# Two transformer blocks on one NeuronCore: GpSimd's block of convolution channels is projected first, and 62 instead of 27 of VectorE's convolution taps stand ahead of the attention

## The chip, the core and the metric

The kernel runs on 1 core of one Trainium2 chip. The time is device microseconds (us) from launch to end. Engines by their names in the profile: PE is TensorE, PEld its weight loads, DVE is VectorE, ACT is ScalarE, POOL is GpSimd, SP is SyncE, which issues most DMAs. Lower is better.

## What is computed

The reference applies two blocks to a sequence of 512 tokens of width 1024, in float32. The change lies in the first mixer of the first block: a gated causal depthwise convolution of 31 taps beside an attention with forget gates.

```python
h = rmsnorm(x, norm_mix_g[l])
proj = h @ w_in[l]
u_glu, q, k, v, f_logit, gate_c, gate_a = jnp.split(proj, cuts, axis=-1)
...
a, gate = jnp.split(u_glu, 2, axis=-1)
u = a * jax.nn.sigmoid(gate)
u = conv(u, dw_w, 31 taps, causal, one filter per channel) + dw_b
u = silu(layernorm(u)) @ pw_w
...
s = q k^T * scale + c_i - c_j        # c: running sum of log sigmoid(f_logit)
p = softmax(s, causal);  o = p @ v   # 8 heads of 64
x = x + (sigmoid(gate_c) * u + sigmoid(gate_a) * (o @ attn_branch_w)) @ w_out
```

After it come a cross attention, a mixture of 16 experts, and a second block with a mixer, a cross attention and a feed-forward layer. None of that is touched.

## The kernel before, in words

Every float32 product is made of three float32r products: a weight chunk (128x1024, brought by DMA to `wraw`) is split into an upper part `wh` (ACT, line 126) and a lower part `wl` (DVE, line 127), and PE multiplies upper by upper, upper by lower and lower by upper (lines 112 to 114). Of `wh` and `wl` there are three buffers each, so that a chunk can be split when PE has done with the chunk three before it. Each projection of 128 columns is 24 such products of 512 columns.

Mixer 1 (`mixer1`) goes through these stages. The norm of the input and the first projections stand in an order written out by hand (`first_norm`). Then come, for each of four blocks `m` of 128 convolution channels, the projections of `a` and of `gate`; ACT takes the tanh of the gate (line 725) and DVE multiplies it with `a` to give `cu` (line 726). The values of the attention follow (four accumulators in PSUM, taken to `v` by ACT and by DVE's line 127), then the forget gates (`fz`, `fc`, lines 754 to 762), then the queries and keys of the first pair of heads, then the attention.

The convolution is made a tap at a time (`conv31`). Three blocks run on DVE: the first tap with the bias is line 919, the other 30 are line 927, each reading `cu` and the sum `acc` and writing `acc`, all in SBUF. Block 3 runs on GpSimd: line 919, and then 30 times a product (line 924, to `pr`) and a sum (line 925, to `acc`). The taps of DVE come from a generator, `taps`, that the code draws on at three places: a number of taps after the forget gates, some in every step of the attention (`some_taps`, after the maximum of that step's scores), and the rest at the end.

The attention has 32 steps (8 heads by 4 blocks of 128 queries), run by `interleave`: a step makes the scores on PE (lines 987 and 988), DVE adds the mask (line 1005), adds the decay and takes the maximum (line 1008), ACT takes the exponential (line 1015), DVE normalises (lines 1017 and 1018), and two steps later PE transposes the result (line 1036). Between the steps PE makes further projections (queries, keys, gates), 14 products to a step.

PSUM has four buffers named `mm` for projections; they go round. The third and fourth accumulators of the values take the buffers of the last block's `a` and `gate`, so that they wait for that block's `cu`.

Outside `first_norm` the rows of each engine are put in order by a scheduler when the kernel is built; every engine then runs its own rows strictly in that order and waits on semaphores. So a row that is late holds up all rows behind it on its engine.

```python
ps0 = first_norm(k, xp, xs, hT, wj, [CU, CU + 512, CU + P])
...
for _ in islice(taps, 27):
    pass
...
def some_taps(s):
    with k.issue_after(k.scored):
        for _ in islice(taps, 2):
            pass
```

Of the kernel before, what the change touches and what calls it, by code (L numbers as in the profile page):

```python
# [27 lines left out]
RAW_BUFS = 4  # weight chunks on their way  # L28
PART_BUFS = 3  # weight chunks in two parts
# [4 lines left out]
class HL:  # L34
    """A float32 value held as the exact sum of two float32r parts."""
# [11 lines left out]
class Stack:  # L47
    """An HL [P, K, T] in tiles of two K each, of the size of a weight chunk."""
# [11 lines left out]
def rev_blocks(ap, n, w=P):  # L60
    """The last dimension (n * w) of a 2-d view, read as n blocks in reverse order."""
    return bass.AP(
        tensor=ap.tensor,
        offset=ap.offset + (n - 1) * w,
        ap=[list(ap.ap[0]), [-w, n], [1, w]],
    )
# [6 lines left out]
class Ctx:  # L73
# [24 lines left out]
    def iota(self, pool, name, shape, pattern, mult):  # L98
        """A float32 tile of base-0 iota values."""
        i = pool.tile(shape, I32, name=name + "i")  # L100
        self.nc.gpsimd.iota(i, pattern=pattern, base=0, channel_multiplier=mult)
        f = pool.tile(shape, FT, name=name)
        self.nc.gpsimd.tensor_copy(f, i)
        return f
# [11 lines left out]
    def mm2(self, out, a, b, first, last):  # L116
        """Products of both parts of b by a, which holds upper and lower parts side by side."""
        nc = self.nc
        nc.tensor.matmul(out, a, b.hi, start=first, stop=False)
        return nc.tensor.matmul(out, a, b.lo, start=False, stop=last)  # L120
# [25 lines left out]
    def ring(self, name, pools):  # L146
        """The next of the pools with its number of buffers, each taken as often as it has them."""
# [8 lines left out]
    def load_w(self, parts, a, c, raws=None, ws=None):  # L156
        """Brings a weight chunk [P, a, c] to the chip, in two parts.

        parts: (slice of the chunk, DRAM view) pairs that together fill it. raws, ws: pools and
        their numbers of buffers to take in turn."""  # L160
# [19 lines left out]
    def load_cols(self, wv, c0):  # L180
        """128 columns of a weight view [P, K, C]."""
        return self.load_w([(None, wv[:, :, c0 : c0 + P])], wv.shape[1], P)

# [19 lines left out]
    def transpose_rows(self, dst, hn, t):  # L203
        """hn [P tokens, D] -> dst[:, j, t-th 128 columns], row p of j holding feature 8p+j."""
# [7 lines left out]
    def turn_job(self, dst, hn, t):  # L212
        """transpose_rows in two steps: the transposes with the upper parts, and the lower parts."""
# [19 lines left out]
    def proj_T(self, w, hT, n):  # L233
        """psum [128 columns of the chunk w, n tokens]."""
# [6 lines left out]
    def proj_job(self, wv, c0, hT, n, evac):  # L241
        """proj_T of 128 columns of a weight view in two halves, then evac(psum)."""
# [14 lines left out]
    def load_rows(self, wv, k0, c0):  # L257
        """Two rows (one at the end of an odd K) and 512 columns of a weight view [P, K, C]."""
# [3 lines left out]
    def proj_rows_job(self, src, nt, wv, evac, pre=(), late=False):  # L262
        """src [P, K, nt*128] (features on partitions) times wv [P, K, C]: evac(t, c0, psum).

        pre: the first chunks, if they have been loaded. late: take the results of 512 columns
        after half of the products of the next."""
# [27 lines left out]
    def proj_x(self, src, wv, mid=None, end=None, also=None):  # L294
        """Adds the products of src [P, K, T] and wv [P, K, D] to x. The last chunks are taken by
        token tile, so that what follows on the first tiles can begin: mid(t) runs after a tile's
        first of these, end(t) after its last. also: a job to do after some of the first
        products."""
# [24 lines left out]
    def proj_norm_head(self, src, wv, g, pool, dst, cols, also=None):  # L323
        """proj_x, the norm of x with the features on partitions in dst, and head() of that."""
# [27 lines left out]
    def head(self, ws, hT, after={}):  # L352
        """proj_T of a few weight chunks, the first half of the tokens before the second.

        after: what is to run after a half (0, 1) of a chunk (0, ...). The results are left in
        PSUM."""
# [10 lines left out]
    def load_x(self, src):  # L367
        """Brings the residual stream [T, D] on chip."""
# [15 lines left out]
    def mem_norm(self, mem, mem_g, room, short):  # L384
        """The memory, normalised, in two tiles of room(). short(): a tile for a short time."""
# [11 lines left out]
    def mem_turn(self, mT, hns):  # L397
        """Puts the memory to mT with the features on partitions, as a job."""
# [4 lines left out]
    def cross_kv(self, pool, mT, wk, wv):  # L403
        """Keys and values of the memory (512 columns), the values as a job to be done."""
# [23 lines left out]
    def cross_attn(self, pool, src, w_prev, free, kv, gain_ap, wq, hd, more=(), also=None):  # L428
        """Adds the products of src and w_prev to x, and gives the heads' outputs of the
        attention to the memory, in pool(). free: to be called when src has been read. kv() gives  # L430
        keys, values and the job that makes these. more: jobs that can be done meanwhile. also: as
        in proj_x."""
# [108 lines left out]
class MemoryKV:  # L541
    """Keys and values (1024 columns) of the memory mT, left in DRAM, in steps.

    room: a tile [P, M] or [P, 512] for a result on its way."""
# [11 lines left out]
    def split_k(self, lo=None):  # L556
        """Brings and splits the next 128 columns of w_k."""
# [4 lines left out]
    def keys(self, room):  # L562
        """The keys of the columns that have waited longest."""
# [3 lines left out]
    def load_v(self, i0, i1, raw, queue=None):  # L567
        """Brings chunks of w_v."""
# [5 lines left out]
    def split_v(self, n=1, lo=None):  # L574
        """Splits the next chunks of w_v; only PART_BUFS may wait for their products."""
# [17 lines left out]
class RowNorm:  # L593
    """The norm of x by token tiles in steps, with the features on partitions in dst."""
# [19 lines left out]
class Feed:  # L614
    """it, with n items taken before they are needed."""
# [19 lines left out]
def ahead(it, n):  # L635
    """it, with n items taken before they are needed."""
# [8 lines left out]
def interleave(steps, lags, jobs, per_step, done, also=None):  # L645
    """Attention steps with other products between them.

    A step is the jobs that its stages need to be done, and a list of stages, each of which needs
    the results of the one before; stage i is issued lags[i] steps after the first, so that the
    chain between them runs meanwhile. jobs yields what it has issued, in products. also(s) runs  # L650
    in every step."""
# [22 lines left out]
def mixer1(k, wide, late):  # L674
    """The sum of the gated branches; wide() makes its place; late() runs near its end."""
# [4 lines left out]
    with ExitStack() as st:  # L680
        hp = st.enter_context(k.sb("m1h", bufs=1))
        hT = k.pair(hp, [P, KD, T], "hT")
        with k.sb("m1x", bufs=1, side="right") as xp:
            xs = [xp.tile([P, D], FT, name=f"xin{t}") for t in range(NT)]
            with k.tc.manual_schedule(engines={*MANUAL, E.Pool, E.SP}):
                ps0 = first_norm(k, xp, xs, hT, wj, [CU, CU + 512, CU + P])
# [3 lines left out]
        # per-channel vectors of the convolution, brought to [channel, value]  # L690
# [24 lines left out]
        with ExitStack() as s2:  # L715
            ap = s2.enter_context(k.sb("m1a", bufs=1))
            # gated unit, transposed: channels on partitions
            us = []
            for m in range(4):
# [7 lines left out]
                us.append(u)  # L727
# [10 lines left out]
            # values, tokens on partitions  # L738
            vt = Values(k, ap, "v")
            k.proj_rows(hT, NT, wj[:, :, CV : CV + 512], lambda t, c0, ps: vt.put(t, ps))  # L740
            # forget gates: running sum of log sigmoid, negated
# [25 lines left out]
            for _ in islice(taps, 27):  # L767
                pass
# [37 lines left out]
            def some_taps(s):  # L806
                with k.issue_after(k.scored):
                    for _ in islice(taps, 2):
# [5 lines left out]
        with ExitStack() as s3:  # L814
# [4 lines left out]
            def branch(b, src, m0):  # L819
                """Two times 128 output channels of a branch, with their gates."""  # L820
# [6 lines left out]
            # layer norm over the channels: to tokens, normalise, and back  # L827
# [34 lines left out]
            # branches, gates and their sum  # L862
# [11 lines left out]
def first_norm(k, pool, xs, dst, wj, cols):  # L874
    """The norm of the input with the features on partitions in dst, and head() of that."""
# [39 lines left out]
def conv31(k, pool, acc, u, cv, hw, pool_engine):  # L915
    """Causal depthwise convolution along the tokens of u [channels, T], a tap at a time."""
# [15 lines left out]
def layer_norm_rows(k, dst, src, eps):  # L932
    """dst = (src - mean) / sqrt(var + eps) along the 512 columns."""
# [12 lines left out]
class HeadPair:  # L946
    """Queries and keys of two heads of 64, the features of one head after the other's.

    A head's queries are held with the upper parts in its own half of the partitions and the lower
    ones in the other, its keys with the upper parts in both, so that one product takes both parts  # L950
    of the queries by the upper ones of the keys."""
# [31 lines left out]
    def scores(self, h, out, cols):  # L983
        """Queries of the columns cols by the first keys."""
# [46 lines left out]
def put_T(k, PT, p, i):  # L1031
    """p [128 queries of block i, keys up to its end] -> PT[keys, kt*512 + (3-i)*128 + query]."""
# [14 lines left out]
class Values:  # L1047
    """Values [tokens, features] of the heads of 64, for products with both parts at once.

    A head has 128 columns: the upper parts of its features, and the lower ones, which come first  # L1050
    where the head is the second of its pair, so that the upper parts have its features' place."""
# [16 lines left out]
    def product(self, pool, h, PT, dst):  # L1068
        """The weights PT of put_T by the values of head h, to dst [P, 4, T]."""
# [16 lines left out]
RAW2, RAW3 = 4, 3  # more room for expert weight chunks on their way  # L1086
AHEAD = 3  # expert weight chunks split before their use
NOROW = 2048
NBLK = NE + 7  # 1024 assignments, at most 512 to an expert, fill at most 7 blocks beyond the first


def first_max(k, pool, v, pw, name):
    """v [P, NT, 4] -> its maximum [P, NT] and the one-hot of the first place that has it."""
# [982 lines left out]
```

## Time and profile before

| | us |
|---|---|
| median of 3 timed runs (lowest, highest) | 1702.78 (1698.17, 1706.14) |
| profiled execution, first to last instruction (its span) | 1700.9 |
| PE busy in the span | 1639.4 |
| DVE busy | 997.0 |
| ACT busy | 729.6 |
| GpSimd busy | 286.5 |

The profile lists for the one profiled execution its span alone; it lies within the timed runs, 1.9 us under their median. Busy times are the sums of the instructions of an engine. A matmul's time in the profile is longer than the distance to the next, because matmuls are pipelined; what PE loses is read from its idle time. Mixer 1 takes the first 330 us or so of the span.

### The profile page before, as it was taken

The numbers are of one execution on the slowest core, as the hardware profiler recorded it, in microseconds if no ns is written. First come the engines' busy times: TensorE is split into PE (matmuls) and PEld (weight loads), VectorE is DVE, ScalarE is ACT, GpSimd is POOL, SyncE is SP. The second block draws the span as 40 slices with busy tenths as digits, with TensorE's granted clock in tenths as the row PEclk, the third lists the DMA queues.
The fourth block names the chain that finished last, engine by engine and source line by source line (L and its number), as shares of the span: only waits on it lengthen the run. The fifth ranks groups of instructions, "written<-read, shape, count | busy, mean of one in ns | idle before, by whom it ended". The sixth has DMA issues, their size and how long they took to land.

```text
span 1700.9 us, 20779 instructions
## 1 busy us (share of the span) xinstructions
PE 1639.4 (96%) x7806; PEld 1332.9 (78%) x7806; DVE 997.0 (59%) x1502; ACT 729.6 (43%) x1154; POOL 286.5 (17%) x268
## 2 busy tenths in 40 slices
PE   7998999999989998799999999999999999999998
PEld 6866778788778886587777888888888888888886
DVE  5679987666668996848885433335554433333223
ACT  4254543344448996545553322223443322222112
POOL 2399000300042332402220011110000000000000
PEclk9999999999999999799999999999999999999999
DMA  6332323556569997552224233335213233333321
GB/s 187 88 94 63 87 76 105 161 152 219 151 199 292 333 329 261 182 154 74 71 62 137 77 91 103 95 103 176 63 50 112 64 98 91 95 97 101 99 88 62
DMA packets 253507, 218.67 MB, mean 129 GB/s; under 512 B 13871, under 2 KB 216111, under 8 KB 253404
## 3 DMA queue, kind: packets, MB, share of 16 engines
q1 hardware_dynamic: 246636, 204.46, 39.9%
q0 software_dynamic: 4896, 9.45, 1.5%
q10 hardware_dynamic: 1872, 3.41, 0.6%
q8 instruction: 62, 1.02, 0.3%
q14 instruction: 41, 0.34, 0.1%
HBM read 208.87 MB, written 16.79 MB: 133 GB/s over the span
## 4 chain that ended last, share of the span: by engine, by line
PE 53%; DVE 3%; issue 1%; ACT 1%; DMA 1%; POOL 1%; SPq 0%; POOLq 0%; DVEq 0%; ACTq 0%
PE mm L112 17%; PE mm L113 16%; PE mm L114 16%; DVE wl L127 1%; PE s L988 1%; PE s L112 0%; DVE yg L1592 0%; PE pt L1036 0%; DMA wraw<-in_w_in_dram 0%; PE s L113 0%; PE s L114 0%; DVE hn L606 0%; DMA wsr<-in_w_spatial_dram 0%; ACT wh L126 0%; PE mm L120 0%
## 5 line engine op out<-in xcount | busy, mean ns | idle before, releaser
L127 DVE TENSOR_TENSOR wl<-wraw,wh 128x1024 fp32r<-128x1024 f32 (+1 forms) x337 | 414.2, 1242 | 364.4 <-ACT wh L126 358.8
L126 ACT ACTIVATE wh<-wraw 128x1024 fp32r<-128x1024 f32 x350 | 356.6, 1029 | 604.9 <-PE mm L113 317.9
L112 PE MATMUL mm<-hT2h,wh 128*128 128x512 f32 (+1 forms) x408 | 160.0, 392 | 0.0
L114 PE MATMUL mm<-hT2h,wl 128*128 128x512 f32 (+1 forms) x408 | 156.1, 383 | 0.0
L113 PE MATMUL mm<-hT2l,wh 128*128 128x512 f32 (+1 forms) x408 | 156.0, 382 | 0.0
L112 PE MATMUL mm<-fhTh,wh 128*128 128x512 f32 (+1 forms) x376 | 143.8, 382 | 0.0
L113 PE MATMUL mm<-fhTl,wh 128*128 128x512 f32 (+1 forms) x376 | 143.7, 382 | 0.0
L114 PE MATMUL mm<-fhTh,wl 128*128 128x512 f32 (+1 forms) x376 | 143.6, 382 | 0.0
L112 PE MATMUL mm<-hTh,wh 128*128 128x512 f32 (+1 forms) x280 | 110.4, 394 | 0.0
L113 PE MATMUL mm<-hTl,wh 128*128 128x512 f32 (+1 forms) x280 | 106.2, 379 | 0.1
L114 PE MATMUL mm<-hTh,wl 128*128 128x512 f32 (+1 forms) x280 | 106.4, 380 | 0.0
L112 PEld LDWEIGHTS mm<-hT2h,wh 128*128 128x128 f32 x408 | 77.2, 189 | 20.0 <-issue 3.4
L114 PEld LDWEIGHTS mm<-hT2h,wl 128*128 128x128 f32 x408 | 77.0, 189 | 16.4
L113 PEld LDWEIGHTS mm<-hT2l,wh 128*128 128x128 f32 x408 | 77.2, 189 | 14.8
L114 PEld LDWEIGHTS mm<-fhTh,wl 128*128 128x128 f32 x376 | 70.9, 189 | 15.1
L113 PEld LDWEIGHTS mm<-fhTl,wh 128*128 128x128 f32 x376 | 70.9, 188 | 15.1
L112 PEld LDWEIGHTS mm<-fhTh,wh 128*128 128x128 f32 x376 | 70.8, 188 | 15.1
L927 DVE SCALAR_TENSOR_TENSOR acc<-cu,hw,acc 128x511 f32<-128x511 f32 (+14 forms) x90 | 71.0, 789 | 0.9
L113 PE MATMUL mm<-wl,gTh 128*128 128x512 f32 x176 | 69.6, 396 | 0.0
L114 PE MATMUL mm<-wh,gTl 128*128 128x512 f32 x176 | 69.6, 395 | 0.0
L112 PE MATMUL mm<-wh,gTh 128*128 128x512 f32 x176 | 69.6, 395 | 0.0
L112 PEld LDWEIGHTS mm<-hTh,wh 128*128 128x128 f32 x280 | 53.5, 191 | 14.1 <-issue 3.4
(469 smaller groups left out, 3583.8 us busy)
## 6 DMA issues: line engine op xcount, KB each, us to landing
wraw<-in_w_in_dram SPq DMA_DIRECT2D x92, 512.0 KB, 4.1
wraw<-in_expert_w_gate_dram SPq DMA_DIRECT2D x64, 256.0 KB, 8.6
wraw<-in_expert_w_up_dram SPq DMA_DIRECT2D x64, 256.0 KB, 8.5
wraw<-in_expert_w_down_dram SPq DMA_DIRECT2D x32, 512.0 KB, 9.1
wraw<-in_w_gate_ffn_dram SPq DMA_DIRECT2D x22, 512.0 KB, 4.2
wraw<-in_w_up_ffn_dram SPq DMA_DIRECT2D x22, 512.0 KB, 4.1
wraw<-in_w_down_ffn_dram SPq DMA_DIRECT2D x22, 512.0 KB, 3.8
wraw<-in_w_out_dram SPq DMA_DIRECT2D x16, 512.0 KB, 4.1
```

What stands on the lines that cost most here:

```text
L112: nc.tensor.matmul(out, a.hi, b.hi, start=first, stop=False)
L113: nc.tensor.matmul(out, a.hi, b.lo, start=False, stop=False)
L114: return nc.tensor.matmul(out, a.lo, b.hi, start=False, stop=last)
L126: a = nc.scalar.activation(dst.hi, src, AF.Copy)
L127: b = (lo or nc.vector).tensor_tensor(dst.lo, src, hi, op=OP.subtract)
L927: yield nc.vector.scalar_tensor_tensor(acc[:, s:], u[:, :n], w, acc[:, s:], op0=OP.mult, op1=OP.add)
L988: nc.tensor.matmul(out, q[own, :], self.kl[own, :n], start=False, stop=True)
```

## The change

Three things are changed, all in `mixer1`. Block 3, the one of GpSimd, is projected first, so that its `cu` is the first to be there; the blocks of DVE follow. Of DVE's 93 taps, 62 (all of blocks 0 and 1) are drawn after the forget gates instead of 27. A step of the attention draws 1 tap instead of 2. (The diff also takes out all comments and docstrings, which moves no instruction; behind line 766 the lines of the changed kernel are one higher.)

```diff
-                ps0 = first_norm(k, xp, xs, hT, wj, [CU, CU + 512, CU + P])
+                ps0 = first_norm(k, xp, xs, hT, wj, [CU + 3 * P, CU + 512 + 3 * P, CU])
...
-            us = []
-            for m in range(4):
+            us = {}
+            for m in (3, 0, 1, 2):
...
-                us.append(u)
+                us[m] = u
...
-            for _ in islice(taps, 27):
+            for _ in islice(taps, 2 * 31):
                 pass
...
-                    for _ in islice(taps, 2):
+                    for _ in islice(taps, 1):
```

What the scheduler makes of it: DVE's rows behind the first `cu`, where the convolution begins. `acc_393` is the sum of block 0, `acc_394` that of block 1. Before:

```order
L726 SCALAR_TENSOR_TENSOR cu<-cu,mm 128x512
...
L729 TENSOR_SCALAR hw<-cv 128x124
L919 TENSOR_SCALAR acc_393<-cu,hw,cv 128x512
L127 TENSOR_TENSOR wl<-wraw,wh 128x1024
L927 SCALAR_TENSOR_TENSOR acc_393<-cu,hw,acc_393 128x511
L927 SCALAR_TENSOR_TENSOR acc_393<-cu,hw,acc_393 128x510
```

Now, in the same place:

```order
L726 SCALAR_TENSOR_TENSOR cu<-cu,mm 128x512
...
L729 TENSOR_SCALAR hw<-cv 128x124
L127 TENSOR_TENSOR wl<-wraw,wh 128x1024 x2
L726 SCALAR_TENSOR_TENSOR cu<-cu,mm 128x512
L920 TENSOR_SCALAR acc_393<-cu,hw,cv 128x512
L928 SCALAR_TENSOR_TENSOR acc_393<-cu,hw,acc_393 128x511
L928 SCALAR_TENSOR_TENSOR acc_393<-cu,hw,acc_393 128x510
```

The first `cu` now belongs to GpSimd's block; DVE's first tap has moved behind two more weight splits and the second `cu`.

The second place is DVE's rows from the second value accumulator on to the first query (line 968, now 969), which opens the attention. Before:

```order
L127 TENSOR_TENSOR wl<-wraw,wh 128x1024 x3
L127 TENSOR_TENSOR v<-mm,v 128x4x128 x4
L127 TENSOR_TENSOR wl<-wraw,wh 128x1024
L755 TENSOR_TENSOR fz<-mm,fz 8x512
L760 SCALAR_TENSOR_TENSOR fz<-fz,fe 8x512
L762 SCALAR_TENSOR_TENSOR fc<-one,fz 8x512
L127 TENSOR_TENSOR wl<-wraw,wh 128x1024
L968 SCALAR_TENSOR_TENSOR q_864<-mm,q_864 64x512
```

Now:

```order
L127 TENSOR_TENSOR v<-mm,v 128x4x128
L928 SCALAR_TENSOR_TENSOR acc_393<-cu,hw,acc_393 128x483
L127 TENSOR_TENSOR v<-mm,v 128x4x128
L928 SCALAR_TENSOR_TENSOR acc_393<-cu,hw,acc_393 128x482
L928 SCALAR_TENSOR_TENSOR acc_394<-cu,hw,acc_394 128x495
L127 TENSOR_TENSOR v<-mm,v 128x4x128
...
L127 TENSOR_TENSOR wl<-wraw,wh 128x1024
L928 SCALAR_TENSOR_TENSOR acc_394<-cu,hw,acc_394 128x482
L969 SCALAR_TENSOR_TENSOR q_899<-mm,q_899 64x512
L980 TENSOR_TENSOR kl<-mm,kh_901 64x512
L969 SCALAR_TENSOR_TENSOR q_900<-mm,q_900 64x512
L1006 TENSOR_TENSOR s<-s,mask 128x128
```

All 62 taps now stand ahead of the first query, between the splits, the values and the forget gates; before, 27 did, and none of them behind the last block's `cu`. Between the first tap and the first query DVE has 82 rows now: 62 taps (60 on line 928; of these 13 follow a tap of the same sum directly, and 47 do not), 10 splits `wl`, and 10 others. On PE only a few rows move: the first product of scores stands behind 441 instead of 433 of the projections' products.

## Rows read from the trace of the kernel before

**Rows 1.** The page's head and part 1: busy time of each engine.

```profile
span 1700.9 us, 20779 instructions
...
PE 1639.4 (96%) x7806; PEld 1332.9 (78%) x7806; DVE 997.0 (59%) x1502; ACT 729.6 (43%) x1154; POOL 286.5 (17%) x268
```

**Rows 2.** By stretch: its length, busy us (count) of PE, PEld, DVE, ACT, POOL, clock.

```profile
36.00:104.00 68.00, 68.00 (x293) 53.28 (x292) 44.54 (x55) 22.67 (x29) 34.57 (x24) 1.00 0.36 97
104.00:168.40 64.40, 55.92 (x242) 41.01 (x242) 62.77 (x127) 31.65 (x64) 60.99 (x38) 1.00 0.28 75
168.40:258.00 89.60, 89.60 (x406) 69.75 (x405) 81.64 (x208) 46.61 (x99) 0.00 (x0) 1.00 0.29 80
```

**Rows 3.** Waits of PE from 104 to 168.4 us: total, times, longest.

```profile
PE pt L1036 <- DVE sc L1018: 5.9, 5, 2.5
PE pt L1036 <- DVE nm L1013: 2.0, 1, 2.0
```

**Rows 4.** Taps of line 927 by stretch: length, DVE busy (count).

```profile
104.00:168.40 64.40, 22.05 (x23) 1.00 0.28 75
183.00:258.00 75.00, 24.92 (x35) 1.00 0.29 81
```

**Rows 5.** Normalising rows of line 1018 by stretch, as in rows 4.

```profile
104.00:168.40 64.40, 10.52 (x12) 1.00 0.28 75
183.00:258.00 75.00, 6.08 (x16) 1.00 0.29 81
```

**Rows 6.** DVE's timeline at the first taps: start, us, line, operation.

```profile
36.99 0.55 DVE L919 TENSOR_SCALAR acc<-cu,hw,cv 128x512 f32<-128x512 f32 x1
...
43.17 1.22 DVE L127 TENSOR_TENSOR wl<-wraw,wh 128x1024 fp32r<-128x1024 f32 x1
44.31 0.68 DVE L726 SCALAR_TENSOR_TENSOR cu<-cu,mm 128x512 f32<-128x512 f32 x1
```

**Rows 7.** PE's timeline at the first product of scores.

```profile
104.08 0.33 PE L987 MATMUL s<-kh,q 128*128 128x128 f32 x1
```

**Rows 8.** GpSimd's timeline: first taps, and first and last in the attention (19 pairs).

```profile
67.43 0.77 POOL L919 TENSOR_SCALAR acc<-cu,hw,cv 128x512 f32<-128x512 f32 x1 [45.52 <-DVE cu L726]
...
71.25 1.57 POOL L924 TENSOR_SCALAR pr<-cu,hw 128x510 f32<-128x510 f32 x1
...
74.09 1.57 POOL L924 TENSOR_SCALAR pr<-cu,hw 128x509 f32<-128x509 f32 x1
...
103.89 2.39 POOL L924 TENSOR_SCALAR pr<-cu,hw 128x500 f32<-128x500 f32 x1
...
167.00 1.34 POOL L925 TENSOR_TENSOR acc<-acc,pr 128x482 f32<-128x482 f32 x1
```

**Rows 9.** DVE's timeline where GpSimd runs at the same time (see rows 8 and 10).

```profile
71.37 1.65 DVE L127 TENSOR_TENSOR wl<-wraw,wh 128x1024 fp32r<-128x1024 f32 x1 [4.06 <-ACT wh L126]
...
154.26 1.41 DVE L927 SCALAR_TENSOR_TENSOR acc<-cu,hw,acc 128x497 f32<-128x497 f32 x1
155.59 1.21 DVE L127 TENSOR_TENSOR wl<-wraw,wh 128x1024 fp32r<-128x1024 f32 x1
...
966.39 2.35 DVE L127 TENSOR_TENSOR wl<-wraw,wh 128x1024 fp32r<-128x1024 f32 x1
...
1152.33 2.32 DVE L127 TENSOR_TENSOR kv0l<-kvr,kv0h 128x1024 fp32r<-128x1024 f32 x1
```

**Rows 10.** GpSimd's timeline at the last three places of rows 9.

```profile
155.23 2.86 POOL L924 TENSOR_SCALAR pr<-cu,hw 128x485 f32<-128x485 f32 x1
...
966.37 1.29 POOL L1853 TENSOR_TENSOR gt<-gt,gt 128x512 f32<-128x512 f32 x1 [37.22 <-DVE gt L1851]
...
1151.23 2.34 POOL L1853 TENSOR_TENSOR gt<-gt,gt 128x512 f32<-128x512 f32 x1 [7.17 <-DVE gt L1851]
```

**Rows 11.** PE by stretch around an idle time in the expert layer: busy (count), granted clock.

```profile
490.00:495.00 5.00, 0.82 (x16) 0.77 1.02 315
495.00:500.00 5.00, 5.00 (x27) 0.54 0.92 240
```

## The prediction

> **What bounds the kernel now.** I read the page's busy times first. PE is busy for 1639.4 of 1700.9 us [rows 1], so the end moves only with what PE waits for, and the reader should look for PE's idle time by stage. The view by stretch [rows 2] splits mixer 1 into three. From 36 to 104 us (projections and forget gates) PE has no idle time: 68.00 of 68.00. From 104 to 168.4 us (the first part of the attention) it is busy for 55.92 of 64.40, so 8.5 us are lost. From 168.4 to 258 us it loses nothing. The view of PE's waits [rows 3] puts 7.9 us of that loss on DVE: the transposes of the probabilities (L1036) stand waiting for rows that DVE has not reached. In that stretch DVE is busy for 62.77 of 64.40; in the one behind it, with the same work and GpSimd silent, for 81.64 of 89.60, and PE does not wait. What differs is GpSimd: 60.99 us busy in the one, none in the other [rows 2]. A tap of DVE takes 22.05/23 = 0.96 us in the first and 24.92/35 = 0.71 in the second [rows 4]; a normalising row 10.52/12 = 0.88 against 6.08/16 = 0.38 [rows 5]. So the loss has two sources, two taps per step and GpSimd's convolution, and the change touches both. At most 8.5 us can come back, 0.5%.
>
> **The attention's taps.** One tap less per step takes about 12 of the 23 taps out of the first stretch: 12 x 0.96 = 11.5 us of DVE's 62.8 [rows 2, 4]. That leaves 51.3 of 64.4, or 80%. At 81.64/89.60 = 91% PE did not wait at all [rows 2], so I credit the whole 8.5 us. If only the part under the full engine came back it could be 6; I take 8.5.
>
> **The front, without GpSimd.** The 35 taps go to the stretch before. DVE has 68.0 - 44.5 = 23.5 us of idle time there [rows 2]; 35 x 0.71 = 25 us come in [rows 4]. So the cover is used up to the last microsecond, before any contention. To see when DVE reaches the attention I walk its new order. It can begin with the taps when the second `cu` is made, at 44.31 + 0.68 = 45.0 us [rows 6]: PE's products ahead of it are as many as before. From there to the first query are 82 rows: 62 taps by 0.71 = 44.0 us [rows 4]; 10 splits by 1.14, the distance of a split to the next row at 43.17 [rows 6], 11.4 us; and 10 small ones, which I price at 0.6 each as the `cu` there (0.68, overlapping the next), 6 us. The sum is 61.4 us, so the first query at 106.4. Two queries, a key and the mask stand until the first maximum, some 1.8 us more: 108. PE's first product of scores stood at 104.08 [rows 7]; 8 more products are ahead of it now, at 68.0/293 = 0.23 us each [rows 2], so 106. DVE is 2 us late. The bounds are 0 (rows of two different sums overlap a little) and 3. Before, this order left DVE idle; now every delay of DVE here is one of PE, since splits, values and queries wait behind the taps in one queue. The first to bite should be the last `cu`: the third accumulator of the values needs the buffer that it frees.
>
> **GpSimd, 30 us earlier.** GpSimd's first tap waited 45.5 us for its `cu` and began at 67.43 [rows 8]. That `cu` is now the first, and the factors `hw` are there at 37.0 [rows 6], so it begins 30 us earlier. Its 30 pairs then run beside DVE's taps from the first to the last of the 62, where before the 27 ahead of the attention all stood ahead of GpSimd's `cu` and met nothing. What one meeting costs is in the trace: a split that comes 0.02 us behind a sum of GpSimd takes 2.35 us instead of 1.22, 1.13 more [rows 6, 9, 10]; one that comes 0.12 us behind a product takes 1.65, 0.43 more [rows 8, 9]. A pair can so cost DVE up to 1.56 us. Bounds for the whole:
> - From below, if GpSimd always gives way: nothing.
> - By the mean of a tap in rows 4: 62 x (0.96 - 0.71) = 15 us.
> - By pairs, scaled: in the first stretch of the attention taps and normalising rows lost 23 x 0.25 + 12 x 0.50 = 11.7 us to 19 pairs [rows 4, 5, 8], 0.62 us a pair, while they would have filled (16.3 + 4.6)/64.4 = 32% of the time. Now the taps alone fill 44.0/61.4 = 72%, 2.2 times as much: 1.36 us a pair. A pair takes 74.09 - 71.25 = 2.84 us nearly undisturbed and (168.34 - 103.89)/19 = 3.39 in the attention [rows 8]; the excess of 0.55, scaled too, makes 4.05. With W the sum lost, (61.4 + W)/4.05 x 1.36 = W gives W = 31.
> - From above, every pair at its full 1.56 us: the same equation gives 39.
>
> I take 25, between the second and the third: the stretch is denser than the attention, but in a run of taps without a gap GpSimd does not always get in. Both happen: the sum at 1151.23 held up the second of two adjoining splits (2.32 us), while the product at 155.23 was passed over by a split that adjoined a tap (1.21 us) and took 2.86 us itself [rows 9, 10].
>
> The Trainium skill ("SBUF — State Buffer", Who interferes with whom) says that a VectorE instruction with two SBUF inputs and a GpSimd instruction that reads SBUF exclude each other, and that whoever is first holds the port for the whole instruction. That it is exclusive the trace bears out (1.13 us of a sum's 1.29); for a product it does not, where 0.43 of 1.57 us were felt. By the rule to the letter the sum would end at rival 4's 1782.
>
> **TensorE's clock.** Waits of several us in one piece may cost more than themselves: in the expert layer PE was busy for 0.82 of 5 us, and in the next 5 us its granted clock was 0.54, near the lower of its two levels [rows 11]. That is 0.46 x 5 = 2.3 us lost there. Mixer 1 has none of it now (1.00 throughout [rows 2]). I take 1 us; bounds 0 and 3.
>
> **The sum.** -8.5 + 2 + 25 + 1 = +19.5 us. The profiled execution (1700.9) lies 1.9 us under the median of the runs, 1702.8, so I add to the median: 1722.3.
>
> **Rivals.**
> 1. *GpSimd gives way* (the other side). If DVE's runs of taps keep the port, W is small. It decides at 6.5, where -8.5 + 2 + W is nothing; from W = 0 and no lateness to that point the time is 1694 to 1703. For it speaks the split at 155.59 [rows 9]; against it the one at 1152.33 and the tap's mean of 0.96 us, which is all from a DVE that was itself full. Chance 0.18.
> 2. *Half of it.* W between 6.5 and 15: the loss ahead of the attention and the gain in it nearly cancel, 1703 to 1711. This is also where it ends if part of the wait overlaps ACT's chain of the forget gates. Chance 0.16.
> 3. *The forecast.* W between 15 and 39, clock 0 to 3: 1711 to 1738. Chance 0.60.
> 4. *More than that.* If GpSimd kept DVE out for the whole of its rows, a pair would cost 1.29 + 1.57 = 2.86 us [rows 8, 10] and the 30 pairs up to 86: 1702.8 - 8.5 + 2 + 86 = 1782. Against it stands the split at 71.37 [rows 9]. A smaller part of that, or an attention that still waits because it starts late, also ends over 1738. Chance 0.06.
>
> That the change does not do what it says is excluded by the order of the rows for DVE; GpSimd's start hangs on nothing but `cu` and `hw` [rows 8].
>
> **How the numbers follow.** A measurement of this kernel (1698.2 to 1706.1 in three runs) can tell about 0.5%, 8.5 us, so "the same" is 1694.3 to 1711.3. Faster needs nearly the whole of the 8.5 us and no price at all, the lower end of rival 1: 0.06. The rest of rival 1 and rival 2 are the same: 0.28. The forecast and rival 4 are slower: 0.66. For the range I cut rival 1 at 1699 (0.10 below) and the forecast at 1735 with rival 4 (0.09 above): 1699 to 1735. The likeliest case has its own range, 1711 to 1738.
>
> **What would show it.** Right: GpSimd's first tap at 37 us and its last near 150; taps ahead of the attention at over 0.9 us in the mean, like those of the first stretch in rows 4; PE idle time between 60 and 130 us, with waits for DVE's `cu`, `v` and `q` or `kl`, of 20 to 30 us together; the first product of scores near 130 us; no idle time of PE in the attention behind it. Wrong: taps at 0.71 to 0.75 us with GpSimd's rows stretched (rival 1), or PE busy throughout from 36 us on. If the taps are slow and PE still does not wait, my walk of DVE's queue is at fault; if PE waits in the attention as before, the two sources of the loss were not the ones I named.

## The result

The changed kernel takes 1717.6 us in the median of four runs (1717.0 to 1718.5), the kernel before, timed beside it, 1700.8: a ratio of 1.0098, interval 1.0077 to 1.0119. It is slower by 13 to 20 us. The prediction said 1722.3, in 1699 to 1735.

The page's head and part 1 of the kernel after: PE is busy 2.7 us longer than in [rows 1], with as many products, and the span is 14.4 us longer, so most of the loss is idle time of PE.

```profile
span 1715.3 us, 20781 instructions
...
PE 1642.1 (96%) x7806; PEld 1333.5 (78%) x7806; DVE 1010.1 (59%) x1502; ACT 729.0 (43%) x1154; POOL 297.5 (17%) x268
```

The view by stretch of the kernel after (columns as in [rows 2]). The first row was 68.00 of 68.00 before:

```profile
36.00:104.00 68.00, 53.83 (x221) 42.56 (x220) 62.43 (x63) 14.49 (x18) 63.38 (x39) 0.91 0.23 64
104.00:168.40 64.40, 58.83 (x233) 42.31 (x234) 57.63 (x109) 29.61 (x53) 42.63 (x23) 0.91 0.34 91
168.40:258.00 89.60, 89.60 (x406) 69.53 (x405) 71.24 (x189) 48.09 (x100) 0.00 (x0) 1.00 0.29 78
```

The waits of PE from 36 to 300 us in the kernel after (total, times, longest): 19.7 us, and all stand ahead of the attention. The waits of [rows 3] are gone.

```profile
PE mm L112 <- DVE cu L726: 7.5, 1, 7.5
PE mm L119 <- DVE v L127: 6.9, 1, 6.9
PE s L988 <- DVE q L969: 4.7, 1, 4.7
PE mm L114 <- DVE wl L127: 0.6, 1, 0.6
```

GpSimd's timeline after, its first tap and its last sum: it begins 30 us earlier than in [rows 8] and needs 111 us instead of 101.

```profile
37.26 1.78 POOL L920 TENSOR_SCALAR acc<-cu,hw,cv 128x512 f32<-128x512 f32 x1 [15.29 <-DVE hw L729]
...
147.19 1.44 POOL L926 TENSOR_TENSOR acc<-acc,pr 128x482 f32<-128x482 f32 x1
```

Two marks serve below to follow the loss. One is DVE's first maximum of scores (106.34 us before), the other PE's transposes for the layer norm behind the attention (264.90 before). DVE's and PE's timelines after have:

```profile
133.26 0.29 DVE L1009 CUSTOM_DVE_ANT_0 sc<-s,negc 128x128 f32<-128x128 f32 x1
```
```profile
282.78 0.62 PE L837 MATMUL s<-ident,acc 128*128 128x128 f32 x4
```

So 26.9 us are lost up to the first maximum, and 9.0 come back in the attention: 17.9 us at the end of the attention. Some 1.9 us of either number (8 x 0.23, an estimate from [rows 2]) are no loss and no gain: they are the eight products that now stand ahead of the scores and no longer behind them.

### The profile page after: what moved, and what is told of

Same layout as the page of the kernel before. It is cut to its first block, busy times and chain, and to the rows that moved or that the text cites. A ratio compares the mean times of both kernels' runs of the same rounds, so it can differ in the third digit from the quotient of the medians.

```text
span 1715.3 us, 20781 instructions
## 1 busy us (share of the span) xinstructions
PE 1642.1 (96%) x7806; PEld 1333.5 (78%) x7806; DVE 1010.1 (59%) x1502; ACT 729.0 (43%) x1154; POOL 297.5 (17%) x268
## 3 DMA queue, kind: packets, MB, share of 16 engines
q8 instruction: 62, 1.02, 0.2%
## 4 chain that ended last, share of the span: by engine, by line
PE 53%; DVE 3%; issue 1%; ACT 1%; DMA 1%; POOL 1%; SPq 0%; POOLq 0%; DVEq 0%; ACTq 0%
PE mm L112 17%; PE mm L114 16%; PE mm L113 16%; DVE wl L127 1%; PE s L989 1%; PE s L112 0%; DVE yg L1593 0%; PE pt L1037 0%; DMA wraw<-in_w_in_dram 0%; PE s L113 0%; PE s L114 0%; DVE hn L606 0%; DMA wsr<-in_w_spatial_dram 0%; ACT wh L126 0%; PE mm L120 0%
## 5 line engine op out<-in xcount | busy, mean ns | idle before, releaser
L113 PEld LDWEIGHTS mm<-hT2l,wh 128*128 128x128 f32 x408 | 76.7, 188 | 14.9
L928 DVE SCALAR_TENSOR_TENSOR acc<-cu,hw,acc 128x511 f32<-128x511 f32 (+22 forms) x90 | 86.6, 986 | 0.5
```

The lines of the kernel that those rows point to most:

```text
L113: nc.tensor.matmul(out, a.hi, b.lo, start=False, stop=False)
L928: yield nc.vector.scalar_tensor_tensor(acc[:, s:], u[:, :n], w, acc[:, s:], op0=OP.mult, op1=OP.add)
```

## The experiments

Theory A is the prediction's: DVE is late because GpSimd's rows meet its dense run of taps. Theory B: 62 taps are too many for DVE there, with or without GpSimd. C and D are named where they are tested. Marks and waits of all kernels, each from one profiled execution; the waits are PE's from 30 to 300 us. Each ratio is against the kernel before timed beside that kernel, whose median was 1700.0 to 1702.0 us:

| kernel | first maximum | layer norm | waits of PE | median us | ratio to before (interval) |
|---|---|---|---|---|---|
| before | 106.34 | 264.90 | 8.4 | 1700.8 | |
| after | 133.26 | 282.78 | 19.7 | 1717.6 | 1.0098 (1.0077 to 1.0119) |
| e1 no GpSimd convolution | 107.55 | 255.41 | 0.4 | 1691.5 | 0.9944 (0.9927 to 0.9961) |
| e2 hint to start GpSimd late | 133.24 | 282.77 | 21.2 | 1719.1 | 1.0099 (1.0080 to 1.0118) |
| e3 block first alone | 117.00 | 269.89 | 10.1 | 1705.2 | 1.0017 (1.0006 to 1.0029) |
| e4 taps moved alone | 118.74 | 270.02 | 11.3 | 1704.6 | 1.0014 (1.0000 to 1.0027) |
| e5 GpSimd behind the taps | 107.71 | 258.96 | 3.0 | 1693.1 | 0.9959 (0.9946 to 0.9971) |
| e6 all four blocks on DVE | 106.46 | 254.99 | 0.2 | 1691.2 | 0.9951 (0.9934 to 0.9968) |
| e7 before, no GpSimd convolution | 105.83 | 255.09 | 0 | 1691.6 | 0.9950 (0.9935 to 0.9965) |
| e8 before, one tap per step | 105.91 | 256.87 | 1.5 | 1692.5 | 0.9953 (0.9935 to 0.9972) |
| e9 products only on GpSimd | 118.00 | 266.97 | 8.1 | 1701.5 | 1.0000 (0.9986 to 1.0013) |
| e10 sums only on GpSimd | 148.17 | 296.05 | 35.3 | 1732.6 | 1.0187 (1.0158 to 1.0217) |

### e1: the changed kernel without GpSimd's pairs

```
-            for _ in taps.pop(0):
-                pass
+            next(taps.pop(0))
```

> The changed kernel with GpSimd's 30 pairs of the fourth block's convolution left out (its first tap stays), so that part of the output is not computed. Theory A (the loss is GpSimd's rows meeting DVE's 62 taps): the taps ahead of the attention fall from 1.05 us to 0.71-0.75, the first maximum comes near 108 us instead of 133, PE waits 0 to 3 us between 36 and 130, and the time is 8.5 - 2 = 6 us under the kernel before, about 1694 where that takes 1701. Theory B (62 taps are too many for DVE there, GpSimd or not): taps at about 1 us or the first maximum past 120, and a time over 1710.

All of A came, and the time is 10 us under the kernel before rather than 6. The lateness of 2 us, which is not paid (below), explains half of that; the rest stays open. The 62 taps ahead of the attention fit. The costliest groups of DVE up to the first maximum (count | busy us, mean ns), e1 from 45 to 107.6 us first, the kernel after from 45 to 133.3 us second:

```profile
L927 DVE SCALAR_TENSOR_TENSOR acc<-cu,hw,acc 128x511 f32<-128x511 f32 (+29 forms) x60 | 41.4, 730 | 0.5
L127 DVE TENSOR_TENSOR wl<-wraw,wh 128x1024 fp32r<-128x1024 f32 x10 | 12.2, 1218 | 0.1
L127 DVE TENSOR_TENSOR v<-mm,v 128x512 fp32r<-128x512 f32 x4 | 2.7, 687 | 0.4 <-ACT v L126 0.3
```
```profile
L928 DVE SCALAR_TENSOR_TENSOR acc<-cu,hw,acc 128x511 f32<-128x511 f32 (+29 forms) x60 | 63.9, 1102 | 0.5
L127 DVE TENSOR_TENSOR wl<-wraw,wh 128x1024 fp32r<-128x1024 f32 x10 | 14.9, 1487 | 0.0
L127 DVE TENSOR_TENSOR v<-mm,v 128x512 fp32r<-128x512 f32 x4 | 2.7, 677 | 0.0
```

The same 60 taps and 10 splits take 63.9 + 14.9 us beside GpSimd and 41.4 + 12.2 without it, 25.2 us more. The first maximum moves by 133.26 - 107.55 = 25.7 us. In both kernels DVE is busy nearly throughout (87.08 of 88.30 us, and 61.17 of 62.60), so its longer rows are the delay. Theory B falls.

### e2: a hint to begin GpSimd's block late

```
-            for _ in taps.pop(0):
-                pass
...
+            with k.issue_after(tp):
+                for _ in late3:
+                    pass
```

> The changed kernel with all of its work, but GpSimd's block begins only behind the last of the 62 taps. Theory A: no meeting ahead of the attention, so the first maximum near 108 us; GpSimd then runs from about 106 to 207 us beside an attention with one tap per step, in which DVE has room, so PE waits there 0 to 3 us: 2 to 6 us under the kernel before, 1695 to 1699 where that takes 1701. Theory B (DVE overloaded by 62 taps): as the changed kernel, 1.010 times the time before. Theory C (GpSimd's pairs cost DVE the same wherever they stand, and DVE has no room): PE waits of 8 us or more between 106 and 207, and no gain.

This tells nothing between A, B and C, since GpSimd began as early as in the kernel after; its timeline has

```profile
37.23 1.78 POOL L922 TENSOR_SCALAR acc<-cu,hw,cv 128x512 f32<-128x512 f32 x1 [15.16 <-DVE hw L729]
```

The hint (`issue_after`, which asks for an order when the kernel is built) made no wait for GpSimd. What was run is the changed kernel once more, and its 1.0099 repeats the result.

### e3 and e4: each half of the change alone

```
-                ps0 = first_norm(k, xp, xs, hT, wj, [CU, CU + 512, CU + P])
+                ps0 = first_norm(k, xp, xs, hT, wj, [CU + 3 * P, CU + 512 + 3 * P, CU])
```

That line, with the order (3, 0, 1, 2) of the loop, is e3. The other half is e4:

```
-            for _ in islice(taps, 27):
+            for _ in islice(taps, 2 * 31):
...
-                    for _ in islice(taps, 2):
+                    for _ in islice(taps, 1):
```

> Part (a) alone: GpSimd's block is projected first, with 27 taps ahead and two per step as before. Theory A: the 30 pairs meet fewer taps ahead of the attention (DVE fills 36 of 61 us there without them); at some 1.2 us a pair 18 to 20 pairs cost 22 to 24 us, about what DVE has free, so PE waits 0 to 5 us there; GpSimd ends near 140 instead of 168, so the attention still loses about 5 of the 8.5 us. Together 1698 to 1703 where the kernel before takes 1701, no difference that can be told. Theory D (an early GpSimd costs what the whole change costs): 1.010.

> Parts (b) and (c) alone: 62 taps ahead and one per step, the blocks projected in the order of before, so that DVE begins its taps some 8 us earlier than in the changed kernel and GpSimd only behind the last of the four. Theory A: GpSimd meets only the last third of the 62 taps, 8 pairs at 1.36 us, 11 us, of which 8 are covered by the earlier start; the first maximum at 108 to 112 us, PE waits 0 to 5 us ahead of it and 0 to 3 in the attention: 1694 to 1701 where the kernel before takes 1701. Theory B (62 taps are too many for DVE): 1.008 or more, with waits of PE of 15 us or more ahead of the attention.

Theories B and D fall: neither half costs what the whole does. But both came out a little over the numbers of A. In e3 the loss ahead of the attention is one wait of 7.6 us for the last `cu`, where 0 to 5 were expected: DVE had the time, but not before that row. In e4 the first maximum was 118.7 instead of 108 to 112, with a wait for the values, and the attention still waited 4.1:

```profile
PE mm L119 <- DVE v L127: 6.6, 1, 6.6
PE pt L1037 <- DVE sc L1019: 3.3, 3, 1.4
```

The 8 us by which DVE begins earlier in e4 were lost again in two ways. GpSimd met DVE with 14 pairs before the first maximum, and not with the 8 that were expected:

```profile
L926 POOL TENSOR_TENSOR acc<-acc,pr 128x511 f32<-128x511 f32 (+13 forms) x14 | 19.3, 1382 | 1.2
```

And behind PE's wait DVE stands idle in its turn, 3.6 us between 104 and 130 us (busy for 22.45 of 26.00), 2.4 of it for the DMA of the forget gates.

The halves do not add: at the layer norm e3 is 5.0 us behind the kernel before, e4 5.1, both together 17.9. Each leaves one cover in place: e3 has DVE's free time ahead of the attention, e4 has a GpSimd that begins only behind the last `cu`.

### e5: the same work, GpSimd held back by its data

```
-            for _ in taps.pop(0):
-                pass
...
+            hw3 = ap.tile([P, 31], FT, name="hw3")
+            nc.vector.scalar_tensor_tensor(
+                hw3, acc[1][:, T - 31 :], 0.0, hw[:, 3, :], op0=OP.mult, op1=OP.add
+            )
+            for _ in conv31(k, ap, acc[3], us[3], cv[:, 3, :], hw3, True):
+                pass
```

> The changed kernel with all of its work, and GpSimd's factors copied by DVE behind the last of the 62 taps, so that GpSimd's block cannot begin before (in the run before last it began at 37 us all the same). Theory A (DVE is late because GpSimd's rows meet its dense run of taps): the first maximum near 108 us, GpSimd from about 106 to 207 us beside an attention with one tap per step; there 30 pairs at about 0.6 us take 18 of the 20 us that DVE has free, so PE waits 0 to 4 us: 0.994 to 0.999 of the time before. Theory C (a pair costs DVE the same wherever it stands): PE waits of 8 us or more between 106 and 207 and no gain, 1.00 or more. Theory B (62 taps alone): 1.010.

GpSimd now begins at 106.14 us and ends at 203.0. PE waits 3.0 us, and the kernel is faster than before, in the range of A; C falls. The pairs still lengthen DVE's rows there (a split takes 1.49 us against 1.22 in e1), but DVE has the time: it is busy for 86.95 of the 97.00 us from 106 to 203. The whole work of the changed kernel is there: only where the pairs stand is different, and that is worth 1717.6 against 1693.1.

```profile
106.14 0.77 POOL L924 TENSOR_SCALAR acc<-cu,hw,cv 128x512 f32<-128x512 f32 x1 [84.05 <-DVE hw L769]
...
201.81 1.21 POOL L930 TENSOR_TENSOR acc<-acc,pr 128x482 f32<-128x482 f32 x1
```

### e6: the fourth block on DVE too

```
-                conv31(k, ap, acc[m], us[m], cv[:, m, :], hw[:, m, :], m == 3)
+                conv31(k, ap, acc[m], us[m], cv[:, m, :], hw[:, m, :], False)
...
-                    for _ in islice(taps, 1):
+                    for _ in islice(taps, 2):
```

> All four convolution blocks on DVE, GpSimd has none: the fourth block's 31 taps join the chain, 62 ahead of the attention and two per step; nothing is left out. Theory A (a tap costs 0.71 us where GpSimd is silent): DVE can begin the taps with the first block, some 8 us earlier, so it is not late (first maximum near 104 to 108 us); in the attention it is busy to about 91%, as behind 183 us before, where PE did not wait: 0.993 to 0.997 of the time before. Theory B (DVE has no room for more): the 31 more taps are 22 us of work for DVE, and the time is 1.00 or more, with waits of PE in the attention.

With 31 more taps on DVE and none on GpSimd the kernel takes 1691.2 us, 0.5% less than before, and is the fastest version here that leaves nothing out (e5, at 0.9959, can't be told from it). By stretch, e6 from 36 to 104 and 104 to 168.4 us:

```profile
36.00:104.00 68.00, 68.00 (x293) 53.49 (x291) 62.79 (x90) 22.20 (x29) 0.00 (x0) 1.00 0.38 102
104.00:168.40 64.40, 64.22 (x287) 49.05 (x286) 59.58 (x151) 37.13 (x75) 0.00 (x0) 1.00 0.30 80
```

DVE is busy for 59.58 of 64.40 us, 93%, and PE waits for 0.2 us in all.

### e7 and e8: the two sources in the kernel before

e7 is e1's edit in the kernel before; e8 takes one tap per step there and leaves out the taps that are then left over:

```
-                    for _ in islice(taps, 2):
+                    for _ in islice(taps, 1):
...
-            for _ in taps:
-                pass
+            next(taps)
```

> The kernel before with GpSimd's 30 pairs left out (that part of the output is not computed). If GpSimd is a source of the 8.5 us lost in the attention, taps there fall from 0.96 to about 0.71 and the normalising rows from 0.88 to about 0.38 us, DVE gets 12 us free in that stretch and PE does not wait: 8.5 us less, 0.995. If two taps per step are the cause by themselves, 1.000.

> The kernel before with one tap per step, GpSimd as it was, and the taps that are then left over (30 of the third block) left out, so that part of the output is not computed. By the term of the prediction (one tap less per step brings the whole 8.5 us back, GpSimd or not): 0.995, no wait of PE in the attention. If one tap less only gives the part under the full engine: 6 us, 0.9965. If GpSimd is the cause by itself: 1.000.

From the first maximum to the layer norm the kernel before takes 158.6 us, e7 149.3 and e8 151.0. Either cure alone brings 9.3 or 7.6 us, nearly the whole, and they don't add: there were 8.5 to have. Without GpSimd's pairs the rest of the change is worth nothing either way: e1 and e7 reach the layer norm at 255.41 and 255.09 us.

### e9 and e10: what a product and what a sum cost

e9 has GpSimd's sum replaced by another product, e10 the product by a sum:

```
-            yield nc.gpsimd.tensor_tensor(acc[:, s:], acc[:, s:], pr[:, :n], op=OP.add)
+            yield nc.gpsimd.tensor_scalar(acc[:, s:], u[:, :n], w, None, op0=OP.mult)
```
```
-            nc.gpsimd.tensor_scalar(pr[:, :n], u[:, :n], w, None, op0=OP.mult)
-            yield nc.gpsimd.tensor_tensor(acc[:, s:], acc[:, s:], pr[:, :n], op=OP.add)
+            nc.gpsimd.tensor_tensor(pr[:, :n], u[:, :n], u[:, :n], op=OP.add)
+            yield nc.gpsimd.tensor_tensor(acc[:, s:], acc[:, s:], u[:, :n], op=OP.add)
```

> The changed kernel with GpSimd's 30 sums replaced by 30 more products of the same form (one SBUF input), so 60 products and no sum; the fourth block's convolution is then not computed. What a product costs a dense DVE: by the row of before (0.43 us felt of 1.57) and a DVE that is at taps 72% of the time, 0.3 us each; some 45 to 60 of them are met, so the first maximum comes 13 to 19 us later than without GpSimd (107.6), at 121 to 127 us, earlier than with pairs (133.3), and the time is about 1.003 to 1.007. If a product held DVE out for its whole duration (1.57 us, 1.1 each in the mean), the first maximum would be past 150 us and the time over 1.02.

> The changed kernel with GpSimd's 30 products replaced by sums of two SBUF inputs, so 60 sums and no product; the fourth block's convolution is then not computed. By the row of before (1.13 us felt of a sum's 1.29) and a DVE at taps 72% of the time, 0.8 us each, up to 49 us for 60: the first maximum at 145 to 157 us, later than with pairs (133.3), and a time of 1.015 to 1.025. If products and sums cost DVE the same, the first maximum would be near that of the products alone.

The taps of DVE up to the first maximum, e9 and then e10, against 41.4 us without GpSimd:

```profile
L928 DVE SCALAR_TENSOR_TENSOR acc<-cu,hw,acc 128x511 f32<-128x511 f32 (+29 forms) x60 | 51.5, 895 | 0.5
```
```profile
L928 DVE SCALAR_TENSOR_TENSOR acc<-cu,hw,acc 128x511 f32<-128x511 f32 (+29 forms) x60 | 76.9, 1318 | 0.5
```

And GpSimd's rows that meet them, e9 from 45 to 118 us and e10 from 45 to 148.2:

```profile
L926 POOL TENSOR_SCALAR acc<-cu,hw 128x510 f32<-128x510 f32 (+18 forms) x19 | 38.6, 2029 | 0.0
L925 POOL TENSOR_SCALAR pr<-cu,hw 128x509 f32<-128x509 f32 (+17 forms) x18 | 37.0, 2056 | 0.0
```
```profile
L926 POOL TENSOR_TENSOR acc<-acc,cu 128x510 f32<-128x510 f32 (+28 forms) x29 | 46.9, 1616 | 0.2
L925 POOL TENSOR_TENSOR pr<-cu 128x507 f32<-128x507 f32 (+25 forms) x26 | 38.7, 1487 | 0.0
```

The first maximum comes 118.00 - 107.55 = 10.45 us late by 37 products, 0.28 us each, and 148.17 - 107.55 = 40.6 us late by 55 sums, 0.74 each. e10 came as expected. e9 came out under its 13 to 19 us, and its 1.0000 under 1.003 to 1.007, mostly because fewer products were met than the 45 to 60 of the estimate: beside DVE a product takes 2.04 us, not 1.57. A pair is then 0.28 + 0.74 = 1.02 us. In the kernel after GpSimd has 24 products and 24 sums between 45 and 133.3 us, and 24 x 1.02 = 24.5 us against 25.7 measured. So W (the prediction's name for the time that DVE loses to GpSimd's rows) is the sum of these meetings.

## Why the prediction was right, step by step

**The attention, -8.5.** Right. From the first maximum to the layer norm the kernel after takes 149.5 us, 9.0 less than before, and PE does not wait there; 1.9 us of the 9.0 are the eight products, and a clock loss stands against it (below). e7 and e8 bear out both sources; what the prediction did not see is that one cure would have been enough.

**DVE late without GpSimd, +2.** The walk through DVE's queue was good to half a microsecond: 108 forecast, 107.55 in e1. In part that is luck: the first query came 1.3 us sooner than forecast (105.07 for 106.4), and from there to the first maximum it took 2.5 us, not 1.8. As a loss the 2 us were an error: the step set DVE's first maximum (108) against PE's first product of scores (106), and in the kernel before these lie 106.34 - 104.08 = 2.3 us apart. Maximum against maximum, with eight more products ahead, it is 108 against 106.34 + 1.9 = 108.2, so no lateness. PE waits in e1 only once, for 0.4 us, and that in the attention.

**W, +25.** Right, 25.7 by e1. The way to it was less so. The bound of 31 had a pair at 1.36 us and one pair in 4.05 us; the runs show 1.07 us (25.7/24) and one in 3.68 us (88.3/24). And the reason for which 25 was taken, that GpSimd does not always get in where taps adjoin, does not hold. Sixteen adjoining taps of DVE, in the kernel after and then in e1, and GpSimd's rows beside the first:

```profile
86.19 17.23 DVE L928 SCALAR_TENSOR_TENSOR acc<-cu,hw,acc 128x491 f32<-128x491 f32 x16
```
```profile
72.87 10.38 DVE L927 SCALAR_TENSOR_TENSOR acc<-cu,hw,acc 128x491 f32<-128x491 f32 x16
```
```profile
88.93 1.83 POOL L925 TENSOR_SCALAR pr<-cu,hw 128x497 f32<-128x497 f32 x1
90.85 1.15 POOL L926 TENSOR_TENSOR acc<-acc,pr 128x497 f32<-128x497 f32 x1
92.10 1.84 POOL L925 TENSOR_SCALAR pr<-cu,hw 128x496 f32<-128x496 f32 x1
...
101.94 1.82 POOL L925 TENSOR_SCALAR pr<-cu,hw 128x493 f32<-128x493 f32 x1
```

GpSimd nearly keeps its pace: four pairs in 13.01 us, 3.25 each (2.84 undisturbed [rows 8]). The 16 taps take 6.85 us more beside five sums and five products, about 1.4 us a pair: here the price is the 1.36 of the bound, not less. The mean of 1.07 comes from the rest of the stretch, where 19 pairs cost the other 18.9 us. There a split can go ahead undisturbed while a product of GpSimd is drawn out, as in the kernel after:

```profile
85.05 1.21 DVE L127 TENSOR_TENSOR wl<-wraw,wh 128x1024 fp32r<-128x1024 f32 x1
```
```profile
84.69 2.91 POOL L925 TENSOR_SCALAR pr<-cu,hw 128x498 f32<-128x498 f32 x1
```

So it is at some splits that GpSimd did not get in, and not in the run of taps. The bound took its price of 1.36 for the whole stretch, which was too high (its pace of 4.05 made up for part of that), and it was then lowered for a reason that does not hold: that 25 came out is in part luck.

**The clock, +1.** The mechanism was right, its size perhaps a little small. After the wait of 7.5 us PE's products are 0.43 us apart instead of 0.23:

```profile
68.58 0.40 PE L114 MATMUL mm<-wh,hTl 128*128 128x512 f32 x1
76.45 0.79 PE L112 MATMUL mm<-wh,hTh 128*128 128x512 f32 x1 [7.47 <-DVE cu L726]
...
77.47 0.63 PE L114 MATMUL mm<-wh,hTl 128*128 128x512 f32 x1
77.90 0.63 PE L112 MATMUL mm<-wh,hTh 128*128 128x512 f32 x1
```

By stretch of the same kernel the granted clock is 0.50, the lower of the two levels (1.2 of 2.4 GHz), for the 12 products from 76.45 to 81.74 us, and full behind them:

```profile
76.45:81.74 5.29, 5.29 (x12) 4.13 (x13) 5.29 (x5) 1.06 (x1) 5.01 (x4) 0.50 0.33 93
81.74:96.00 14.26, 14.26 (x63) 11.47 (x62) 14.26 (x15) 3.38 (x5) 13.53 (x9) 1.00 0.14 40
```

That is 12 x (0.44 - 0.23) = 2.5 us. It happens behind each of the three long waits (granted clock 0.50 from 103.9 to 109.0 us and from 132 to 136 too). Behind the first two it should cost nothing, since PE then waits again, and the less long, for DVE, which is busy nearly throughout. This is also why PE's waits sum to 19.7 us, just under the 20 to 30 forecast, where DVE is 26.9 late. Behind the third it is on the path; from the first maximum to the layer norm the kernel after is 149.52 - 147.86 = 1.7 us slower than e1, which has no such wait, and I put that down to the clock without a run that isolates it.

**The sum.** +19.5 forecast, +17.9 at the layer norm. The profiled execution ends only 14.4 us later. The code behind the layer norm is the same in all of these kernels, and took 1436.0 us before, 1432.5 after, 1435.6 in e7 and 1429.6 in e8: single executions differ there by 6 us. The medians give 16.8. By e1 the 17.9 are -9.5 us for the attention and the lateness together (-6.5 forecast), 25.7 for W (25) and 1.7 behind the first maximum (1).

**The rivals.** GpSimd giving way (W under 6.5) and half of it (under 15) fall with 25.7. So does the hold for GpSimd's whole rows, which would have put a pair at 2.86 us. The Trainium skill ("SBUF — State Buffer", Who interferes with whom, and Summary: rules for kernel authors) states that hold: of a VectorE instruction with two SBUF inputs and a GpSimd instruction that reads SBUF, the one that issues second is blocked until the first has finished. For the sum the runs come near it, 0.74 us of 1.05 to 1.29; for the product, 0.28 of 1.57, they do not. The Trainium skill (Who interferes with whom) also states that a VectorE instruction with at most one SBUF input, outside VectorE's two-port modes, does not contend with GpSimd. The values' rows (`v`, one input in PSUM) agree: they took 0.677 us in the kernel after, beside taps of 1.10, and 0.687 in e1. The normalising rows, which read one tensor from SBUF and yet went from 0.38 to 0.88 us beside GpSimd [rows 5], would have to be in such a mode; no run here shows whether they are.

## What to carry to other kernels

An engine's free time is spent once: DVE's 23.5 us ahead of the attention could take the 35 taps or GpSimd's meetings, not both, and each half of this change cost little alone (1.0017 and 1.0014). Before work is moved to an engine with free time, walk its new queue in order, and price by the meeting what runs beside it on an engine whose rows lengthen its own. Here 31 more taps on DVE itself (22 us, at the 0.71 of [rows 4]) were cheaper than 30 pairs on GpSimd beside it (25.7 us of DVE's time by 24 of them), and the same pairs cost PE only 3.0 us of waits where DVE has room (e5).

## What was not expected of the hardware

- In a row of 16 adjoining taps on DVE, GpSimd kept a pair in 3.25 us (2.84 undisturbed), and DVE paid about 1.4 us a pair. Over the whole stretch DVE paid 1.07 us a pair, GpSimd some 0.8 (3.68 instead of 2.84).
- A GpSimd product of one SBUF input costs DVE 0.28 us in the mean of the stretch, a sum of two 0.74, though the product lasts longer.
- A wait of 7.5 us cost PE 2.5 us more by its clock, and nothing of it was seen in the time where another wait for the same engine followed.
